# Reading the output projection's operands early, with SyncE in program order in the value slots of a hybrid mLSTM and forgetting-attention layer

## The chip, the cores and the metric

One core of a Trainium2 chip runs the whole layer in one launch. The metric is device time in microseconds, the median of three runs. TensorE is PE here, its weight loads PEld, VectorE DVE, ScalarE ACT, GpSimd POOL, and SyncE, which issues nearly all DMAs of this kernel, SP.

## The reference

A decoder layer on 1024 tokens of width 1024: four mLSTM heads and eight heads of forgetting attention side by side, then cross attention into 256 memory tokens, then a squared-ReLU MLP. The part around the change:

```python
def forgetting_attention(q, k, v, lf):
    ...
    def block(args):
        qi, ci, blk = args
        ...
        s = jnp.einsum('bqhd,bkhd->bhqk', qi, k, preferred_element_type=jnp.float32) * scale
        s = s + (ci[..., :, None] - cT[..., None, :])
        s = jnp.where(qpos[:, None] >= kpos[None, :], s, -jnp.inf)
        p = jax.nn.softmax(s, axis=-1)
        return jnp.einsum('bhqk,bkhd->bqhd', p.astype(v.dtype), v)
...
x = x + jnp.concatenate([ml_out, fx_out], axis=-1) @ w_out[l]
x = x + cross_attention(rmsnorm(x, ln_x[l]), rmsnorm(mem, ln_mem[l]), w_xq[l], w_xkv[l], w_xo[l])
```

## The kernel before

Everything is float32, and nearly every product is made in three passes of a reduced float32 type: each operand is split into a high part and a remainder (`split`: ACT copies the high part, DVE or POOL subtracts), and `mm3` (lines 190 to 194) multiplies low by high, high by low and high by high. PE's program is therefore long and almost without holes.

A planner orders the instructions of each engine before the launch, from estimated times. `in_order` (line 148) overrides it: the instructions traced inside such a block, on the four compute engines, are chained in the order of the program. Those of SP are not among them, so their order is the planner's. Each engine executes its own list strictly in order, and so does SP: an instruction that waits holds all behind it.

The part around the change has three steps.

**Leading slots** (line 1063). `score_parts` (line 833) gives the parts of the forgetting scores: for each of eight heads eight tiles of 128 queries, each tile of one or two parts of at most 512 keys, twelve parts a head. A slot (`slot`, line 998) takes one part: PE multiplies it (`Tile.score`, lines 754 and 755) into one of three `sc` banks. One slot later the mask is added (line 734) and DVE takes the maximum (`top`, line 761); two slots later ACT takes the exponential (`exp`, line 767), which frees the bank; three slots later POOL scales by the denominator (`scale`, line 778). Thirteen such slots run ahead of the value products, beside `token_major` (line 503), which projects the forgetting values in two halves of eight token tiles, and whose sink (line 661) stores them to DRAM (`fvd`).

**Value slots** (line 1076). 96 slots, each with one step of the value products: PE transposes one key tile of the probabilities (line 793), ACT and DVE split it (`cut`), and two slots later PE multiplies it with the values (line 813). In the same slot go the next score part, one read of `coming` (`fx_step`, line 725), stores of finished pairs of heads to `mix` (`fx_store`, lines 828 and 829), and filler work at a rate of 3.6 a slot (`filler`): first keys and values of the memory (`key_unit`, `value_unit`), which read the normalized memory `hm`, from slot 57 on the first part of the output projection (`out_unit`), for both halves of the tokens. The fillers' weights come through two raw buffers: `raw_load` (line 959) reads one, `cut_half` (lines 971 and 972) splits half of one a slot, and the next read into a buffer is issued when its cut is done. `coming` holds the stack reads of the head after next (`fx_load`, eight a head) and the residual `x` into `kept`, two a head.

**Drain** (line 1080). The slots without value products that follow, and then the rest of the filler.

The output projection's operand, `mix` (the outputs of the mLSTM heads and of the pairs of forgetting heads, high part and remainder), goes through DRAM. Units 0 and 4 of the first half read it (lines 927 and 928): four mLSTM heads at once with `mix_load`, two reads of 1 MB into an `act` buffer, of which there are seven, and one pair of forgetting heads with `mix_tile`, two reads of 256 KB into a `z4` buffer.

Of the kernel before, what the change touches and what calls it, by code (L numbers as in the profile page):

```python
# [9 lines left out]
F32 = mybir.dt.float32  # L10
F32R = mybir.dt.float32r
# [5 lines left out]
COMPUTE = (mybir.EngineType.PE, mybir.EngineType.Activation, mybir.EngineType.DVE, mybir.EngineType.Pool)  # L17
P = 128
T = 1024
TH = 512  # L20
D = 1024
KT = D // P
NM = 256
MLH = 4
FXH = 8
# [3 lines left out]
KX = 1  # L29
# [15 lines left out]
def hybrid_layer(ctx: ExitStack, tc: tile.TileContext, a: dict, out: bass.AP):  # L45
# [16 lines left out]
    def act(dt=F32R):  # L62
        return sb("act", [P, 8, TH], 7, dt)
# [12 lines left out]
    def z4():  # L76
        return sb("z4", [P, T + 3], 2)
# [33 lines left out]
    load = nc.sync.dma_start  # L111
# [33 lines left out]
    last_of = {}  # L145

    @contextmanager
    def in_order():

        traced = nc.cur_bb.bb.instructions  # L150
        last = traced[-1]
        yield
        start = next(k for k in reversed(range(len(traced))) if traced[k] is last) + 1
        for i in traced[start:]:
            if i.engine not in COMPUTE:
                continue
            if i.engine in last_of:
                tc.add_manual_dep(
                    i,
                    last_of[i.engine],  # L160
                    mybir.DependencyInfo(mybir.DependencyClass.NoSync, mybir.DependencyReason.DATA),
                    reason="in_order",
                )
            last_of[i.engine] = i.name
# [120 lines left out]
    hmd = dram.tile([P, 2, KT, NM], F32, name="hmd")  # L285
# [49 lines left out]
    for k in range(KT):  # L335
        if k % 2 == 0:
            c = slice(k % 4 * 256, k % 4 * 256 + 512)
# [44 lines left out]
    z, e, q, lf = (small[:, i:j].rearrange("p (t c) -> p t c", c=c) for i, j, c in ((0, 128, GC), (128, 224, GW), (224, 320, GW), (320, 416, GW)))  # L382
# [120 lines left out]
    def token_major(w_src, sink, cs=(0, 1), between={}, ready=()):  # L503

        for c in cs:
            ws = [both(ready.pop(0) if ready else weights(w_src[c, i]), lambda t: t.rearrange("p (k c) -> p k c", k=4)) for i in range(2)]
            for t in range(8):
                if t in between:
                    between[t]()
                hf, tt = divmod(t, 4)  # L510
                ps = mm()[:, 0:256]
                for k in range(KT):
                    x = both(h[hf], lambda z: z[:, k, tt * P : (tt + 1) * P])
                    mm3(ps, x, both(ws[k // 4], lambda z: z[:, k % 4]), k == 0, k == KT - 1)
                sink(t, c, ps)
# [59 lines left out]
    mix = dram.tile([2, 2, P, KT, TH], F32, name="mix")  # L575
# [83 lines left out]
    fvd = dram.tile([FXH, P, 8, 2 * FXD], F32, name="fvd")  # L659
# [6 lines left out]
    closing = iter(())  # L666
# [29 lines left out]
    closing = gates_then_memory()  # L696
    ready = ml_project(0)
    for hd in range(MLH):
        closing = ml_head(hd, *ready)
# [5 lines left out]
    for _ in range(2):  # L705
        t = act().rearrange("p a b -> p (a b)").rearrange("p (i c) -> p i c", i=4)
# [5 lines left out]
    coming = []  # L712
# [19 lines left out]
    def mask():  # L732
        while masks:
            nc.tensor.matmul(masks.pop(0), identb, causal, start=False, stop=True)
# [94 lines left out]
        load(mix[hf, 1, :, MLH + hd // 2], lo.bitcast(F32))  # L829

    rooms = {}

    def score_parts():

        for hd in range(FXH):
            for hf in range(2):
                if hf:
                    t = act(F32).rearrange("p a b -> p (a b)").rearrange("p (i c) -> p i c", i=4)
                    rooms[hd, hf] = [t[:, d, : (5 + d) * P] for d in range(4)]
                else:  # L840
                    t = [w4((P, 2, TH)) for _ in range(2)]
                    rooms[hd, hf] = [t[d // 2][:, d % 2, : (1 + d) * P] for d in range(4)]
                for d in range(4):
                    x = Tile(hd, 4 * hf + d, rooms[hd, hf][d])
                    for e in range(len(x.parts)):
                        yield x, e
            if hd + 2 < FXH:
                fx_load(hd + 2)
            if 0 < hd < 5:
                coming.extend((kept[:, n], a["x"][:, n, :TH]) for n in (2 * hd - 2, 2 * hd - 1))  # L850

    def fv_load(hd):
        t = w4((P, 8, P), F32R)
        load(t.bitcast(F32), fvd[hd])
        return t

    def value_steps():
# [14 lines left out]
    def mix_load(k0, k1, hf):  # L872
        t = act().rearrange("p (e k) c -> p e k c", e=2)
        for p_ in range(2):
            load(t[:, p_, : k1 - k0].bitcast(F32), mix[hf, p_, :, k0:k1])
        return [(t[:, 0, k], t[:, 1, k]) for k in range(k1 - k0)]

    def mix_tile(k, hf):
        t = z4()[:, :T].bitcast(F32R).rearrange("p (e c) -> p e c", e=2)
        for p_ in range(2):  # L880
            load(t[:, p_].bitcast(F32), mix[hf, p_, :, k])
        return t[:, 0], t[:, 1]

    late = []

# [34 lines left out]

        return [a["w_xv"][hd, i] for i in range(2)], run

    mixes = {}

    def out_unit(hf, n):
        def run(ws):
            if n == 0 and hf == 0 or n == 4 and hf == 0:
                mixes[n // 4] = mix_load(0, MLH, n // 4) + [mix_tile(k, n // 4) for k in range(MLH, MLH + KX)]
            x = kept[:, n]
            if hf:  # L930
                x = rotate("p", "b", "a", "p", "b")
                load(x, a["x"][:, n, TH:])
            w = both(ws[0], lambda t: t.rearrange("p (k c) -> p k c", k=MLH + KX))
            ps = mm()
            for k in range(MLH + KX):
                mm3(ps, both(w, lambda t: t[:, k]), mixes[hf][k], k == 0, k == MLH + KX - 1)
                yield 3.0, k == MLH + KX - 1, lambda: sink(x, ps)

        def sink(x, ps):
            v.tensor_tensor(out=x, in0=ps, in1=x, op=ALU.add)  # L940
            if hf:
                load(x1d[:, n], x)

        return [a["w_out_a"][n]], run
# [47 lines left out]
    scored, exped, adds, ended = [], [], [], []  # L992
# [2 lines left out]

    stores, topped = [], []

    def slot(values, until):
        with in_order():
            todo_ = late[:]  # L1000
            late.clear()
            closing = bool(ended)
            sums = []
            while ended:
                sums.append(fx_close(*ended[0]))
                hd, hf, _ = ended.pop(0)
                if hd % 2:
                    stores.append((hd, hf, True))
            x = next(steps_, None) if values else None
            if x:  # L1010
                x.turn()
            mask()

            while adds and not closing and len(adds) >= (LAG if x else 1):
                y = adds.pop(0)
                y.add()
                if y.last:
                    ended.append((y.hd, y.hf, y.ov))
                    break
            tops = scored[:]  # L1020
            scored.clear()
            for t, e in tops:
                t.top(e)
            if x:
                x.cut()
                adds.append(x)
            for f in sums:
                f()
            exps = topped[:]
            topped[:] = tops  # L1030
            for t, e in exps:
                t.exp(e)
            while exped:
                exped.pop(0).scale()
            exped.extend(t for t, e in exps if e == len(t.parts) - 1)
            fx_step()
            part = next(parts, None)
            if part:
                part[0].score(part[1])
                scored.append(part)  # L1040
            late.extend(filter(None, [f() for f in todo_]))
            if stores and stores[0][2]:
                stores[0] = (*stores[0][:2], False)
            elif stores:
                fx_store(*stores.pop(0)[:2])
            while spent[0] < until:
                step = next(fill, None)
                if step is None:
                    break
                spent[0] += step[0]  # L1050
                if step[1]:
                    late.append(step[2])
                    break
            n, e = divmod(halves[0], 2)
            if until and n < len(sources) and (e or sum(u >= now[0] for u, _ in sources[:n]) < 3):
                cut_half()
        return x
# [5 lines left out]
    for i in range(LEAD_):  # L1063
        slot(False, 0)
        if i in (1, 11):
            next(closing, None)
    token_major(a["w_fv"], fv_sink, between={4: lambda: next(closing, None)})
    hm = act().rearrange("p a b -> p (a b)").rearrange("p (e k c) -> p e k c", e=2, k=KT)
    kept = act(F32)
    load(hm.bitcast(F32), hmd)  # L1070
    banks[:] = ["mm", "m2"]
    raw_load()
    raw_load()
# [1 line left out]
    n = 0  # L1075
# [255 lines left out]
    for n in range(KT):  # L1331
# [7 lines left out]
        k = n % 4  # L1339
# [390 lines left out]
```

## Time and profile before

| | us |
|---|---|
| runs shown, median of three (lowest, highest) | 1522.5 (1521.36, 1523.13) |
| the profiled execution, its own time | 1519.66 |
| its span, first to last instruction | 1517.6 |
| PE busy in it | 1501.4 |
| DVE, ACT, POOL busy | 1103.2, 716.6, 438.5 |

An engine's row of the profile has its busy time, its share of the span and its instructions. A row of the waits has who waited, for whom, the total in us, how often, and the longest. A row of the order of time has the start, the duration, engine and line, operation, what is written and read, and in brackets how long the engine had been idle and what ended that. SPq is SP issuing a DMA: the row has the time of the issue, not of the transfer. Idle time below about 0.2 us isn't listed. The clock of PE was granted at 0.998 of its full rate on the mean of this execution.

### The profile page before, as it was taken

What the parts mean: (1) busy time and instruction counts of PE and PEld (TensorE: products, weight loads), DVE (VectorE), ACT (ScalarE), POOL (GpSimd) and SP (SyncE); (2) the same over time, 40 slices, a digit from 0 to 9 for tenths busy, and PEclk for the clock granted to TensorE, in tenths of its full rate; (3) what the DMA queues carried; (4) which work ended last, traced back from release to release, by engine and by line L of the source; (5) the groups of instructions that cost most, each with busy time, mean ns of one, the idle gap of its engine ahead of it and who ended that gap; (6) DMA issues with size and microseconds to landing.
All of it is one profiled execution on the core that took longest, in us unless ns stands there. A gap on an engine that the chain in (4) does not pass through costs nothing.

```text
span 1517.6 us, 21814 instructions
## 1 busy us (share of the span) xinstructions
PE 1501.4 (99%) x7708; PEld 1259.1 (83%) x7708; DVE 1103.2 (73%) x1741; ACT 716.6 (47%) x1345; POOL 438.5 (29%) x497
## 2 busy tenths in 40 slices
PE   9999999999999999999999999999999999999997
PEld 8888888889898888888888887788888888888887
DVE  7676676665798875844457888788887788777765
ACT  7343343334678763543443456565556432222124
POOL 0003030413455541011110033343333544333312
PEclk9999999999999999999999999999999999999999
DMA  6332323436897928634333436776775966555623
GB/s 212 112 115 89 118 100 124 133 125 179 253 296 225 310 89 285 228 108 130 124 110 126 163 122 237 276 276 238 273 254 215 364 260 222 222 222 214 256 85 111
DMA packets 113489, 288.32 MB, mean 190 GB/s; under 512 B 12626, under 2 KB 27276, under 8 KB 107236
## 3 DMA queue, kind: packets, MB, share of 16 engines
q1 hardware_dynamic: 113092, 286.82, 55.4%
q8 instruction: 60, 0.98, 0.3%
q14 instruction: 49, 0.40, 0.1%
q10 hardware_dynamic: 288, 0.11, 0.0%
HBM read 194.36 MB, written 92.53 MB: 189 GB/s over the span
## 4 chain that ended last, share of the span: by engine, by line
PE 61%; DVE 2%; DMA 2%; issue 1%; ACT 1%; POOL 1%; SPq 0%; POOLq 0%; DVEq 0%; ACTq 0%
PE sc L192 5%; PE sc L194 5%; PE sc L193 5%; PE tp L192 5%; PE tp L194 5%; PE tp L193 5%; PE m L193 4%; PE m L192 4%; PE m L194 4%; PE mm L193 4%; PE mm L192 4%; PE mm L194 4%; PE ov L192 2%; PE ov L194 2%; PE ov L193 2%
## 5 line engine op out<-in xcount | busy, mean ns | idle before, releaser
L193 PE MATMUL tp<-act,wh 128*128 128x512 f32 (+1 forms) x456 | 178.7, 392 | 0.0
L192 PE MATMUL tp<-act,wl 128*128 128x512 f32 (+1 forms) x456 | 178.6, 392 | 0.0
L194 PE MATMUL tp<-act,wh 128*128 128x512 f32 (+1 forms) x456 | 178.5, 392 | 0.0
L138 ACT ACTIVATE wh<-wr 128x1024 fp32r<-128x1024 f32 (+3 forms) x96 | 92.7, 967 | 98.4 <-PE tp L194 36.5
L139 DVE TENSOR_TENSOR wl<-wr,wh 128x1024 fp32r<-128x1024 f32 (+3 forms) x96 | 114.3, 1192 | 15.3 <-ACT wh L138 15.2
L192 PE MATMUL mm<-act,wl 128*128 128x512 f32 (+1 forms) x320 | 122.8, 384 | 0.0
L193 PE MATMUL mm<-act,wh 128*128 128x512 f32 (+1 forms) x320 | 122.5, 383 | 0.0
L194 PE MATMUL mm<-act,wh 128*128 128x512 f32 (+1 forms) x320 | 122.2, 382 | 0.0
L192 PE MATMUL m<-act,wl 128*128 128x512 f32 (+1 forms) x312 | 119.6, 383 | 0.3 <-DVE wl L139 0.3
L193 PE MATMUL m<-act,wh 128*128 128x512 f32 (+1 forms) x312 | 119.0, 381 | 0.7 <-DMA act<-mix 0.7
L194 PE MATMUL m<-act,wh 128*128 128x512 f32 (+1 forms) x312 | 119.0, 381 | 0.0
L192 PE MATMUL sc<-act,wl 128*128 128x512 f32 (+1 forms) x268 | 103.9, 388 | 0.0
L193 PE MATMUL sc<-act,wh 128*128 128x512 f32 (+1 forms) x268 | 103.7, 387 | 0.0
L194 PE MATMUL sc<-act,wh 128*128 128x512 f32 (+1 forms) x268 | 103.7, 387 | 0.0
L194 PEld LDWEIGHTS tp<-act,wh 128*128 128x128 f32 x456 | 85.7, 188 | 19.5
L192 PEld LDWEIGHTS tp<-act,wl 128*128 128x128 f32 x456 | 85.7, 188 | 19.1 <-DVE w L1374 0.3
L193 PEld LDWEIGHTS tp<-act,wh 128*128 128x128 f32 x456 | 85.8, 188 | 18.8
L1464 POOL TENSOR_TENSOR z<-wr 128x256 f32<-128x256 f32 x56 | 54.1, 986 | 147.1 <-DMA wr<-w_ff2q 135.2
L138 ACT ACTIVATE w<-wr 128x768 fp32r<-128x768 f32 (+2 forms) x31 | 25.5, 824 | 132.1 <-PE tp L194 69.1
L138 ACT ACTIVATE wh<-z 128x1024 fp32r<-128x1024 f32 (+2 forms) x55 | 52.5, 956 | 65.7 <-POOL z L1464 30.5
L139 DVE TENSOR_TENSOR wl<-z,wh 128x1024 fp32r<-128x1024 f32 (+2 forms) x55 | 65.9, 1199 | 11.3 <-ACT wh L138 11.2
L194 PEld LDWEIGHTS mm<-act,wh 128*128 128x128 f32 x320 | 60.1, 188 | 12.5
(673 smaller groups left out, 4197.3 us busy)
## 6 DMA issues: line engine op xcount, KB each, us to landing
act<-right SPq DMA_DIRECT2D x35, 1024.0 KB
right<-r_d SPq DMA_DIRECT2D x70, 256.0 KB
right<-w SPq DMA_DIRECT2D x56, 256.0 KB
wr<-w_ff2q SPq DMA_DIRECT2D x28, 512.0 KB
act<-fqk SPq DMA_DIRECT2D x48, 256.0 KB
wr<-w_in SPq DMA_DIRECT2D x20, 512.0 KB
wr<-w_ff SPq DMA_DIRECT2D x20, 512.0 KB
fqk<-r_p SPq DMA_DIRECT2D x32, 256.0 KB
```

The source lines that it names most:

```text
L138: s.activation(hi, src, AF.Copy)
L139: return v.tensor_tensor(out=lo, in0=src, in1=hi.bitcast(F32), op=ALU.subtract)
L192: nc.tensor.matmul(ps, w[1], x[0], start=first, stop=False, skip_group_check=more)
L193: nc.tensor.matmul(ps, w[0], x[1], start=False, stop=False, skip_group_check=more)
L194: nc.tensor.matmul(ps, w[0], x[0], start=False, stop=last, skip_group_check=more)
L1464: g.tensor_tensor(out=o, in0=x, in1=y, op=op)
```

## The change

Four edits, all around the slots:

- `in_order` takes the engines that it chains. In the leading and the value slots SP is among them; in the drain it is not.
- `score_steps` is what the slot did with maxima, exponentials and scaling, made a generator. `catch_up` runs it alone, with the mask, ahead of tiles 0 and 2 in both halves of the value projection.
- The reads of `mix` by the output units go into `coming`, one read of 256 KB a slot (`mix_ahead`): the first half's with heads 2, 3 and 4, the second half's with head 6. The residual reads are spread over heads 1, 4 and 5.
- The memory operand `hm`, one read of 2 MB, becomes two of 1 MB; the second is issued behind the first read of forgetting values.

```diff
-    def in_order():
+    def in_order(engines=COMPUTE):
...
-            if i.engine not in COMPUTE:
+            if i.engine not in engines:
...
-            if 0 < hd < 5:
-                coming.extend((kept[:, n], a["x"][:, n, :TH]) for n in (2 * hd - 2, 2 * hd - 1))
+            if hd == FXH - 2:
+                extra[hd].extend(mix_ahead(1))
+            coming.extend(extra[hd])
...
     def fv_load(hd):
         t = w4((P, 8, P), F32R)
-        load(t.bitcast(F32), fvd[hd])
+        x = load(t.bitcast(F32), fvd[hd])
+        if hd == 0:
+            with tc.issue_after(x.ins):
+                load(hm[:, :, KT // 2 :].bitcast(F32), hmd[:, :, KT // 2 :])
         return t
...
-    def mix_tile(k, hf):
-        t = z4()[:, :T].bitcast(F32R).rearrange("p (e c) -> p e c", e=2)
-        for p_ in range(2):
-            load(t[:, p_].bitcast(F32), mix[hf, p_, :, k])
-        return t[:, 0], t[:, 1]
+    mixes = {}
+
+    def mix_ahead(hf):
+        t = act().rearrange("p (e k) c -> p e k c", e=2)
+        z = [z4()[:, :T].bitcast(F32R).rearrange("p (e c) -> p e c", e=2) for _ in range(KX)]
+        mixes[hf] = [(t[:, 0, k], t[:, 1, k]) for k in range(MLH)] + [(y[:, 0], y[:, 1]) for y in z]
+        return [(mixes[hf][k][p_], mix[hf, p_, :, k]) for k in range(MLH + KX) for p_ in range(2)]
...
-            if n == 0 and hf == 0 or n == 4 and hf == 0:
-                mixes[n // 4] = mix_load(0, MLH, n // 4) + [mix_tile(k, n // 4) for k in range(MLH, MLH + KX)]
...
+    def score_steps():
+        tops = scored[:]
+        scored.clear()
+        for t, e in tops:
+            t.top(e)
+        yield
+        exps = topped[:]
+        topped[:] = tops
+        for t, e in exps:
+            t.exp(e)
+        while exped:
+            exped.pop(0).scale()
+        exped.extend(t for t, e in exps if e == len(t.parts) - 1)
+
+    def catch_up():
+        with in_order():
+            mask()
+            for _ in score_steps():
+                pass
+
     def slot(values, until):
-        with in_order():
+        with in_order(COMPUTE + (mybir.EngineType.SP,) * (values or not until)):
...
-    token_major(a["w_fv"], fv_sink, between={4: lambda: next(closing, None)})
+    token_major(a["w_fv"], fv_sink, between={0: catch_up, 2: catch_up, 4: lambda: next(closing, None)})
     hm = act().rearrange("p a b -> p (a b)").rearrange("p (e k c) -> p e k c", e=2, k=KT)
     kept = act(F32)
-    load(hm.bitcast(F32), hmd)
+    residual = [(kept[:, n], a["x"][:, n, :TH]) for n in range(KT)]
+    operands = mix_ahead(0)
+    for hd, more in ((1, residual[:4]), (2, operands[:4]), (3, operands[4:8]), (4, operands[8:] + residual[4:6]), (5, residual[6:])):
+        extra[hd].extend(more)
+    load(hm[:, :, : KT // 2].bitcast(F32), hmd[:, :, : KT // 2])
```

More of the change, by code (lines that the diff above doesn't have):

```diff
@@ L831, in hybrid_layer @@
     rooms = {}
+    extra = [[] for _ in range(FXH)]
     def score_parts():
@@ L921, in value_unit @@
         return [a["w_xv"][hd, i] for i in range(2)], run
-    mixes = {}
     def out_unit(hf, n):
         def run(ws):
-            if n == 0 and hf == 0 or n == 4 and hf == 0:
-                mixes[n // 4] = mix_load(0, MLH, n // 4) + [mix_tile(k, n // 4) for k in range(MLH, MLH + KX)]
             x = kept[:, n]
@@ L1019, in slot @@
                     break
[L1020 to L1023, printed above, removed]
+            going = score_steps()
+            next(going)
             if x:
@@ L1028, in slot @@
                 f()
[L1029 to L1035, printed above, removed]
+            next(going, None)
             fx_step()
```

## The prediction

> **What bounds the kernel now.** I read the page's head first, then the waits of PE between 285 and 600 us, then the busy time of each engine over successive groups of twelve slots, and last the order of time on each engine around every wait of PE.
>
> ```profile
> span 1517.6 us, 21814 instructions
> PE 1501.4 (99%) x7708; PEld 1259.1 (83%) x7708; DVE 1103.2 (73%) x1741; ACT 716.6 (47%) x1345; POOL 438.5 (29%) x497
> ```
>
> PE is busy for all but 16.2 us. The edits touch neither a product of PE nor its order, so they can only give back idle time of PE, or add to it. In the part that they touch, this is all of it that the profile lists:
>
> ```profile
> PE sc L754 <- ACT act L767: 2.5, 2, 1.8
> PE tp L793 <- DVE r_e L139: 1.5, 2, 0.9
> PE m L193 <- DMA act<-mix: 0.7, 1, 0.7
> PE sc L754 <- ACT w L767: 0.4, 1, 0.4
> PE tp L793 <- DVE w L139: 0.3, 1, 0.3
> ```
>
> The sum is 5.4 us. It is a ceiling on what can be gained from waits that the profile shows.
>
> ```profile
> L793 PE MATMUL tp<-ident,act x208: 270/272/329, 395.9 to 576.4; 128*128 128x128 f32 x104
> L793 PE MATMUL tp<-ident,w x80: 270/273/329, 391.3 to 563.5; 128*128 128x128 f32 x80
> 391.00:414.00 23.00, 21.03 (x154) 19.18 (x153) 19.75 (x46) 17.98 (x50) 10.74 (x17) 1.00 0.72 218
> 414.00:437.00 23.00, 22.93 (x175) 21.64 (x174) 20.83 (x50) 19.19 (x53) 12.85 (x18) 1.00 0.98 309
> 437.00:464.00 27.00, 24.96 (x185) 22.91 (x184) 23.33 (x56) 19.89 (x57) 13.97 (x21) 1.00 0.85 261
> 464.00:488.00 24.00, 24.00 (x186) 22.88 (x183) 21.07 (x51) 19.68 (x54) 12.82 (x20) 1.00 0.75 210
> 488.00:513.00 25.00, 23.69 (x166) 21.50 (x165) 21.86 (x58) 19.04 (x55) 13.68 (x24) 1.00 0.95 300
> 513.00:536.00 23.00, 23.00 (x135) 19.50 (x134) 19.22 (x46) 16.34 (x49) 11.43 (x19) 1.00 0.88 272
> 536.00:559.00 23.00, 23.00 (x135) 19.40 (x134) 20.05 (x49) 17.00 (x50) 10.77 (x18) 1.00 0.29 90
> ```
>
> The transposes of the probabilities (L793) mark the 96 value slots: from 391.3 to 576.4, about 1.94 us a slot. The windows are groups of about twelve slots; their columns are PE, PEld, DVE, ACT and POOL busy, clock, DMA share and GB/s. PE loses time in three of them: 2.0 us at the start, 2.0 us in the third, 1.3 us in the fifth. DVE is 84 to 91% busy throughout, the next bound once PE's waits are gone.
>
> **The change part by part.**
>
> *Leftover scores (catch_up).* Thirteen leading slots leave behind one mask and one maximum, the exponentials of the last two score parts and the scaling of two tiles. Today the first value slots do them:
>
> ```profile
> 388.71 0.47 ACT L141 ACTIVATE r_c<-tp,rcol 128x256 fp32r<-128x256 f32 x1 [2.59 <-DMA mix<-r_e]
> 391.54 0.47 ACT L141 ACTIVATE r_b<-m,rcol 128x256 fp32r<-128x256 f32 x1 [2.35 <-PE m L194]
> 391.78 0.29 DVE L761 TENSOR_REDUCE c_mx<-sc 128x1 f32<-128x128 f32 x1 [2.07 <-PE sc L734]
> 392.53 0.68 ACT L767 ACTIVATE act<-sc,c_mx 128x512 f32<-128x512 f32 x1
> 393.10 0.20 ACT L767 ACTIVATION_READ_ACCUMULATOR act<-sc,c_mx 128x1 f32 x1
> 393.20 0.29 ACT L769 ACTIVATE c_mx<-c_mx 128x1 f32<-128x1 f32 x1
> 393.36 0.44 PE L754 MATMUL sc<-act 128*128 128x384 f32 x1 [0.73 <-ACT act L767]
> 393.75 0.37 ACT L767 ACTIVATE w<-sc,c_mx 128x128 f32<-128x128 f32 x1
> 397.15 0.39 PE L754 MATMUL sc<-act 128*128 128x256 f32 x1 [0.38 <-ACT w L767]
> ```
>
> PE's next scores need one of three banks and wait 0.73 and 0.38 us for exponentials to free them. Moved beside the value projection, ACT's share (0.68 + 0.20 + 0.29 + 0.37 us, and a second accumulator read of about 0.20) is 1.7 us. ACT has idle stretches of 2.59 and 2.35 us there, and DVE one of 2.07, so nothing waits for it. Without that cover it would cost at most those 1.7 us, in front of the projection's sinks. I take a gain of 0.73 + 0.38 = 1.11 us; bounds: a loss of 1.7, and a gain of 2.0, all that the first window has.
>
> *SP in program order.* At present SP's order is the planner's. The largest wait of PE comes out of it:
>
> ```profile
> 448.49 0.86 DVE L972 TENSOR_TENSOR wl<-wr,wh 128x512 fp32r<-128x512 f32 x1 [0.37 <-ACT wh L971]
> 449.88 0.32 SPq L829 DMA_DIRECT2D mix<-r_f  x1
> SPq L881 <- DMA mix<-r_y: 2.4, 1, 2.4
> 452.65 0.32 SPq L881 DMA_DIRECT2D z<-mix  x1
> 453.07 0.37 SPq L959 DMA_DIRECT2D wr<-w_xv  x1
> 453.05 0.26 ACT L767 ACTIVATION_READ_ACCUMULATOR act<-sc,c_mx 128x1 f32 x1
> 457.06 0.63 ACT L971 ACTIVATE wh<-wr 128x512 fp32r<-128x512 f32 x1 [3.75 <-DMA wr<-w_xv]
> 458.68 0.50 PE L754 MATMUL sc<-act 128*128 128x512 f32 x1 [1.77 <-ACT act L767]
> ```
>
> The buffer of the raw weights was free at 448.49 + 0.86 = 449.35, yet w_xv is issued only at 453.07. In front of it stood the early read of the forgetting operand (z<-mix), waiting 2.4 us for the store of what it reads. ACT, in order, then sits 3.75 us at the weight cut, the exponentials behind it are late, and PE stands 1.77 us. In the changed order that read is no longer there (it moves to slots 56 and 57); w_xv follows the store of 449.88 and goes out near 450.3. With the same 3.99 us from issue to cut (453.07 to 457.06) the cut starts near 454.3, after a wait of about 1.0 us. Of the 3.75 us PE felt 1.77, so 1.98 us was slack, and 1.0 stays under it. Gain 1.77 us. What is late next is the remaining 0.26 + 0.65 us of waits for DVE, which I leave. Bounds: a gain of 2.7 (those too), and a loss by new stops of SP, priced with the rivals.
>
> The order also puts behind each waiting SP instruction whatever follows it in its slot: stack reads, stores of the memory keys and values, reads of raw weights. The stores wait for DVE and ACT work of the same slot, which stands ahead of the weight cut in DVE's own order too, so a raw read is not held by them: its buffer comes free later still. A stack read has about four slots, 8 us, before PE wants it.
>
> *Output operands early.* Twenty reads of 256 KB take the place of four of 1024 and four of 256, one a slot: the first half in slots 32 to 35, 44 to 47, 56 and 57, the second in 72 to 81.
>
> ```profile
> 422.71 3.15 SPq L728 DMA_DIRECT2D act<-x  x6
> 498.93 1.34 SPq L875 DMA_DIRECT2D act<-mix  x2
> 521.87 1.60 SPq L875 DMA_DIRECT2D act<-mix  x2
> 508.63 0.50 PE L193 MATMUL m<-act,wh 128*128 128x512 f32 x1 [0.67 <-DMA act<-mix]
> ```
>
> PE waits 0.67 us for the two reads issued at 498.93; in the new order their content has landed ten slots and more before. That is a gain of 0.67 us. The tightest piece is the forgetting operand, read in slots 56 and 57 and used in slot 60: three slots, 5.8 us, against the 3.99 us above. One slot late would cost 1.9, the other bound. Twelve more issues at about 0.35 us are 4 us of SP over 185, hidden. The bytes stay the same, but 4 MB leave the fifth and sixth window, where DMA was at 0.95 and 0.88, half of them for the third and fourth window (0.85 and 0.75), half for the seventh (0.29). The residual reads, six of them one after the other at 422.71 in the fullest window (0.98), spread out. PE was 22.93 of 23 busy there, so I book nothing.
>
> *Memory operand in two reads.*
>
> ```profile
> 377.90 0.56 SPq L1070 DMA_DIRECT2D act<-hmd  x1
> ```
>
> No wait of PE names it: issued at 377.90, first used after slot 4 begins near 396. The second read costs one more issue of 0.56 us on SP. Zero, and 0.56 either way.
>
> *Sum.* 1.11 + 1.77 + 0.67 = 3.55 us. The profiled execution took 1519.66 us, its span and 2.1 around it, and would take 1516.1; the median of the runs shown is 2.8 above it, so I forecast 1522.5 - 3.55 = 1519.0.
>
> **The rivals.**
>
> *SP becomes the head of the line (slower).* Place: raw reads (L959) in the value slots. If the strict order makes SP stop for a buffer or a landing ahead of a raw read, as z<-mix did, every such stop costs what that one cost, 1.77 us. Two eat the gain, four end at 1522.5 - 3.55 + 7.08 = 1526.0. For it: two raw buffers only, ACT in order, and by the code sixteen raw reads of key and value weights in the slots. Against: the waits in program order follow DVE's own order, as above.
>
> *DVE takes the time back.* At 84 to 91% DVE is close. If each of the three recoveries returns half as waits like the two of 0.9 us under r_e, the gain is 1.8 and the time 1520.7.
>
> *The leftovers are not done earlier.* If DVE and ACT reach them only when the projection ends, 1.11 is lost: 1520.1.
>
> *The smaller reads crowd the raws.* At 309 GB/s (window 414 to 437) 256 KB take 0.85 us of all DMA engines. Two of them ahead of a raw read in slots 32 to 47 raise ACT's wait from 1.0 to 2.7, 0.7 over the slack; at two places, 1.4: gain 2.1, 1520.4. [...]
>
> *More than the listed waits.* All 5.4 us go: 1517.1.
>
> **How the numbers follow.** Forecast 0.44, its own range 1517.5 to 1520.2; more 0.14; SP at the head of the line 0.17; DVE 0.12; leftovers 0.06; crowding 0.07. About 0.2%, 3.0 us, is what a measurement of this kernel can tell from no change: faster means under 1519.5, slower over 1525.5. Faster: 0.35 of the forecast's 0.44 and all of "more", 0.49. Slower: 0.14 of the SP rival's 0.17. The rest, 0.37, is the same. Range 1516.2 to 1524.5: below lies what unlisted gaps of PE could add to 5.4, above lies most of the SP rival.
>
> **What would show it.** Leftovers: the exponentials of the last leading parts stand before 391 and no score of the first six slots waits. SP order: no wait of ACT for w_xv over 2 us, and no z<-mix before slot 56. Operands: no wait of PE for mix. Wrong would be: a longer sum of PE's waits in the slots, ACT waiting for wr in several places, or idle time of PE under r_e beyond 1.5 us.

## The result, and the profile after

| | us, median (lowest, highest), runs | before beside it | ratio, 95% interval |
|---|---|---|---|
| the changed kernel | 1524.59 (1520.2, 1530.4), 22 | 1522.05 (1518.88, 1525.28), 22 | 1.0016 [1.0008, 1.0023] |

The change makes the kernel 2.5 us slower by the medians, where 3.5 us of gain had been forecast. The profiled execution took 1524.3 us, against 1519.66 before. The head of the profile after:

```profile
span 1522.6 us, 21823 instructions
PE 1502.7 (99%) x7708; PEld 1260.8 (83%) x7708; DVE 1098.4 (72%) x1741; ACT 717.2 (47%) x1345; POOL 444.8 (29%) x497
```

The waits of PE in it between 285 and 600 us:

```profile
PE sc L754 <- ACT act L767: 6.9, 3, 4.0
PE tp L793 <- DVE r_e L139: 0.4, 1, 0.4
PE tp L793 <- DMA act<-fqk: 0.3, 1, 0.3
PE tp L793 <- DVE w L139: 0.3, 1, 0.3
PE mm L192 <- DVE r_b L943: 0.2, 1, 0.2
```

Two waits of before are gone: the one for `mix` (0.7) and those for the leftover exponentials. But scores behind an exponential (L754 <- L767) now wait 6.9 us, not 2.5, so the listed sum rises from 5.4 to 8.1 us. Three of the groups of slots, in the columns of the rows before:

```profile
391.00:414.00 23.00, 19.95 (x146) 18.14 (x145) 17.25 (x38) 15.73 (x43) 8.65 (x13) 1.00 0.87 240
437.00:464.00 27.00, 22.70 (x169) 21.10 (x168) 21.17 (x48) 17.93 (x51) 13.45 (x20) 0.99 0.89 240
464.00:488.00 24.00, 24.00 (x173) 22.71 (x173) 19.72 (x52) 18.57 (x53) 11.88 (x19) 0.94 0.83 237
```

PE loses 3.1 us in the first (2.0 before) and 4.3 in the second (2.0). In the last it is busy throughout but does 173 matmuls, not 186: the granted clock is 0.94 there. The order of time on ACT, SP, DVE and PE around the two stalls of the changed kernel:

```profile
387.57 0.54 SPq L856 DMA_DIRECT2D w<-fvd  x1
388.16 0.61 SPq L859 DMA_DIRECT2D act<-hmd  x1
...
388.94 0.36 ACT L767 ACTIVATE w<-sc,c_mx 128x128 f32<-128x128 f32 x1
...
398.03 1.56 SPq L728 DMA_DIRECT2D act<-fqk  x2
401.81 0.36 SPq L962 DMA_DIRECT2D wr<-w_xk  x1
408.48 0.63 ACT L974 ACTIVATE wh<-wr 128x512 fp32r<-128x512 f32 x1 [3.62 <-DMA wr<-w_xk]
410.10 0.50 PE L754 MATMUL sc<-act 128*128 128x512 f32 x1 [2.63 <-ACT act L767]
...
449.98 0.86 DVE L975 TENSOR_TENSOR wl<-wr,wh 128x512 fp32r<-128x512 f32 x1 [0.36 <-ACT wh L974]
450.45 0.38 SPq L856 DMA_DIRECT2D w<-fvd  x1
450.88 0.46 SPq L728 DMA_DIRECT2D act<-fqk  x1
451.45 0.53 SPq L962 DMA_DIRECT2D wr<-w_xv  x1
460.83 0.63 ACT L974 ACTIVATE wh<-wr 128x512 fp32r<-128x512 f32 x1 [6.02 <-DMA wr<-w_xv]
462.45 0.50 PE L754 MATMUL sc<-act 128*128 128x512 f32 x1 [4.04 <-ACT act L767]
```

The last leftover exponential stands at 388.94, before 391 as forecast. Both stalls are raw weight reads that land late. w_xv goes out 0.6 us after its buffer is free (449.98 + 0.86 = 450.84), which is what the forecast wanted of the new order; but from issue to cut it takes 9.38 us, against 3.99 before. w_xk takes 6.67 us (401.81 to 408.48), and it is a wait that before did not have. Ahead of each stand reads of values and stacks, 512 and 256 KB each, and ahead of w_xk the first read of values and half of the memory operand too, issued at 387.57 and 388.16. While w_xk was on its way the DMA engines were full (in these rows the last two columns are the DMA share and GB/s):

```profile
402.00:406.00 4.00, 4.00 (x29) 3.65 (x27) 3.93 (x7) 2.62 (x8) 1.29 (x1) 1.00 1.03 214
```

In the kernel before, the same stretch had this:

```profile
402.00:406.00 4.00, 4.00 (x28) 3.62 (x28) 3.93 (x7) 3.38 (x9) 1.29 (x1) 1.00 0.42 138
```

### The profile page after: what moved, and what is told of

The parts are those of the page before. It is cut to its first block, busy times and chain, and to the rows that moved or that the text cites. A ratio compares the mean times of both kernels' runs of the same rounds, so it can differ in the third digit from the quotient of the medians.

```text
span 1522.6 us, 21823 instructions
## 1 busy us (share of the span) xinstructions
PE 1502.7 (99%) x7708; PEld 1260.8 (83%) x7708; DVE 1098.4 (72%) x1741; ACT 717.2 (47%) x1345; POOL 444.8 (29%) x497
## 4 chain that ended last, share of the span: by engine, by line
PE 87%; DVE 4%; DMA 4%; ACT 2%; issue 2%; POOL 1%; SPq 0%; POOLq 0%; DVEq 0%; ACTq 0%
PE tp L194 8%; PE tp L193 8%; PE tp L192 8%; PE m L192 6%; PE m L194 6%; PE m L193 6%; PE sc L192 6%; PE sc L194 6%; PE sc L193 6%; PE mm L192 5%; PE mm L193 5%; PE mm L194 5%; PE ov L192 2%; PE ov L193 2%; PE ov L194 2%; PE ov L813 2%
```

## The experiments

Each is a whole kernel, run beside the kernel before. A difference of 0.001 between ratios is 1.5 us.

**Taking the change apart.** e1: the changed kernel with SP's order left to the planner.

```diff
-        with in_order(COMPUTE + (mybir.EngineType.SP,) * (values or not until)):
+        with in_order():
```

> The changed kernel with SP's order in the slots left to the planner again; operands early, leftovers beside the value projection and the memory operand in two reads stay. Theory (program order of SP interleaves stack reads with raw weight reads, so that raw reads land late: 9.4 and 6.6 us instead of 4.0 and 3.4): the two PE waits of 2.6 and 4.0 us under the exponentials shrink to under 2 us together, the leftovers' 1.1 us stay won, and the time is 1 to 3 us below before and 3 to 6 below the changed kernel. Rival (the 256 KB operand reads crowd the raw reads whoever orders them): the waits near slots 33 to 36 stay over 3 us and the time is that of the changed kernel, 2 to 3 us above before.

Measured: 1522.94, ratio 1.0004 [0.9995, 1.0014]. From its order of time:

```profile
388.52 0.34 SPq L856 DMA_DIRECT2D w<-fvd  x1
395.21 0.73 PE L813 MATMUL ov<-r_e,w 128*128 128x512 f32 x1 [1.83 <-DMA w<-fvd]
```

Without SP's order the wait for w_xk is gone but PE waits for the first read of values, a wait that neither kernel has. Its issue is as late as in the changed kernel, so SP's order isn't what makes it late. The longest wait of PE that is left, 3.5 us, is the one behind w_xv: in the planner's order three of the operand reads (act<-mix, from 452.73) go out ahead of it, and it takes 5.88 us from issue to cut (455.02 to 460.90). So the theory's "under 2 us together" missed, and in this order the operand reads do crowd a raw read, as the rival has it.

e2: the kernel before, with SP in program order in the slots and nothing else of the change:

```diff
...
-        with in_order():
+        with in_order(COMPUTE + (mybir.EngineType.SP,) * (values or not until)):
```

> The kernel before with one edit: SP chained in program order in the leading and value slots; operands still read at the output units, 1 MB at a time. Theory: raw reads behind stack reads land late here too; PE waits under the exponentials of 4 us or more in all, 2 to 5 us above before. Rival (256 KB operand reads crowd the raws): no operand read before slot 56, so no long wait there, and the time is that of before or 1 to 2 us below it, since the early read that blocked SP at 450 is gone.

Measured: 1531.91, ratio 1.0058 [1.0046, 1.0070]. Its two longest waits of PE, in order of time:

```profile
514.85 0.77 PE L192 MATMUL m<-act,wl 128*128 128x512 f32 x1 [5.20 <-DMA act<-mix]
517.59 0.80 PE L193 MATMUL m<-act,wh 128*128 128x512 f32 x1 [1.97 <-DMA act<-mix]
```

In program order the bulk reads of `mix` go out (at 508.77) right ahead of their first use, and PE stands 7.2 us, which neither expectation named; under the exponentials it waits 2.9 us in all, where the theory had 4 or more. So the order costs time without the early operands. That it gains time with them is not shown by itself: e4 and e6 below, without and with it, are at 0.9991 and 0.9985, e7 and e8 at 0.9986 and 0.9982, and in both pairs the intervals overlap.

e3: the kernel before with the early leftovers (`score_steps`, `catch_up` and the new `between`) alone:

```diff
...
+    def catch_up():
+        with in_order():
+            mask()
+            for _ in score_steps():
+                pass
...
-    token_major(a["w_fv"], fv_sink, between={4: lambda: next(closing, None)})
+    token_major(a["w_fv"], fv_sink, between={0: catch_up, 2: catch_up, 4: lambda: next(closing, None)})
```

> The kernel before with one edit: the leftover scores finished beside the first value tiles. Theory: no wait of PE in the first two value slots, 1.1 us less idle time of PE there, 0.5 to 1.1 us below before. Rival (the leftovers displace the projection's sinks and the planner's order behind them): the same or 1 to 2 us above before.

Measured: 1528.64, ratio 1.0040 [1.0028, 1.0052]. From its order of time:

```profile
392.16 0.34 SPq L854 DMA_DIRECT2D w<-fvd  x1
399.39 0.80 PE L813 MATMUL ov<-r_e,w 128*128 128x512 f32 x1 [4.22 <-DMA w<-fvd]
```

The part that was forecast at +1.1 us of gain is the one that loses. The first read of values goes out at 392.16; PE waits 4.22 us for it. The rival had the direction, but not the size: by the ratio it is 6.1 us, not 1 to 2.

e4: the kernel before with the early operands and the spread residual alone:

```diff
-            if n == 0 and hf == 0 or n == 4 and hf == 0:
-                mixes[n // 4] = mix_load(0, MLH, n // 4) + [mix_tile(k, n // 4) for k in range(MLH, MLH + KX)]
...
+            if hd == FXH - 2:
+                extra[hd].extend(mix_ahead(1))
+            coming.extend(extra[hd])
```

> The kernel before with one edit: operands of the output projection and residual in the paced list, in 256 KB reads; SP's order is the planner's, the leftovers stay in the value slots, the memory operand is one read. Theory: PE's 0.67 us wait for mix is gone; the rest depends on where the planner puts the reads; within 1 us of before. Rival (256 KB reads crowd the raws): 2 us or more above before, with ACT waits for raw weights over 4 us.

Measured: 1520.87, ratio 0.9991 [0.9981, 1.0000]. The wait for `mix` is gone; the 0.67 us forecast for it lie inside the interval (0 to 2.9 us).

**The late first read of values.** Four kernels take the leftovers apart. e6: the changed kernel without `catch_up`:

```diff
-    token_major(a["w_fv"], fv_sink, between={0: catch_up, 2: catch_up, 4: lambda: next(closing, None)})
+    token_major(a["w_fv"], fv_sink, between={4: lambda: next(closing, None)})
```

> The changed kernel without the early leftovers (no catch_up), all else as in it. If the early leftovers are worth what the forecast gave them (1.1 us) here too: waits of 0.7 and 0.4 us come back at the first scores, the 4.04 us for w_xv stays between 3 and 4.5, and the time is 1525 to 1526.5. Rival, the early exponential takes a buffer the first value read needs, that read and the memory operand go out late and push w_xk's read: w<-fvd is issued near 371 instead of 387.6, the 2.63 us for w_xk falls to 1.0 or less, and the time is 1522.5 to 1523.7.

Measured: 1519.2, ratio 0.9985 [0.9975, 0.9996]: the rival was right in what it says of the reads, and the time is 3 us below its range. From its order of time:

```profile
449.21 0.53 SPq L962 DMA_DIRECT2D wr<-w_xv  x1
456.45 0.63 ACT L974 ACTIVATE wh<-wr 128x512 fp32r<-128x512 f32 x1 [3.70 <-DMA wr<-w_xv]
```

No wait of PE for w_xk is left, and the first read of values goes out at 370.28 again. The early leftovers cost the changed kernel 0.0031 of its time, 4.7 us. The wait for w_xv is as large as before: 3.70 us of ACT, 1.72 of PE.

e7: e4 with only the first of the two leftover steps (SP's order is the planner's). The exponential of part 12, the only one that writes a tile of the second forgetting head, stays in the first value slot:

```diff
...
+    caught = []
+
     def catch_up():
+        if caught:
+            return
+        caught.append(1)
         with in_order():
...
-    token_major(a["w_fv"], fv_sink, between={0: catch_up, 2: catch_up, 4: lambda: next(closing, None)})
+    token_major(a["w_fv"], fv_sink, between={0: catch_up, 4: lambda: next(closing, None)})
```

> Early operands alone (as in e4) with one of the two early leftover steps: the exponential of part 12, the only one that writes a buffer of the second forgetting head, stays in the first value slot. Theory, that exponential took the buffer which the first value read was to have: w<-fvd is issued near 371 as before, PE has no wait for it (4.22 us in e3, 1.83 in e1), the 0.73 us wait at the first scores goes, that of 0.38 may stay; time 1519.8 to 1520.5, e4 was 1520.9. Rival, the early leftovers delay that read in another way, by the work they move: a wait of 1.8 us or more for w<-fvd with half clock behind it stays, and the time is 1523 to 1528.

Measured: 1520.02, ratio 0.9986 [0.9977, 0.9995]; w<-fvd is issued at 371.56, no wait for it, none at the first scores. e8: the same edit on the whole changed kernel:

> The changed kernel with the exponential of part 12 left in the first value slot (the other early leftover steps stay). Theory, this one exponential takes the buffer of the first value read and so delays that read by 17 us and the memory operand's second half, the next stacks and w_xk behind it: w<-fvd is issued near 371, w_xk's read lands in under 4 us, the 2.63 us for w_xk is gone, no wait at the first scores but at most 0.4; time 1518.5 to 1520, e6 was 1519.2 with 0.7 more of waits there. Rival, the early leftovers cost time because the slots start in another phase against the reads: w<-fvd goes out early but the waits for w_xk and w_xv stay over 5 us in sum, time 1522.5 to 1525.

Measured: 1518.97, ratio 0.9982 [0.9973, 0.9991]. w<-fvd goes out at 370.45 and the wait for w_xk is gone. In e7 and e8 the first read and the time came out as the theory has them. Leaving one 0.36 us exponential where it was gives the changed kernel back 5 us.

Is it the exponential, or its place in the program? e11: the changed kernel, all leftovers early again, but the first read of values stands in the program ahead of that exponential:

```diff
+    def early_steps():
+        catch_up()
+        yield
+        first.append(fv_load(0))
+        catch_up()
+
+    first, early = [], early_steps()
-    token_major(a["w_fv"], fv_sink, between={0: catch_up, 2: catch_up, 4: lambda: next(closing, None)})
+    token_major(a["w_fv"], fv_sink, between={0: lambda: next(early, None), 4: lambda: next(closing, None)})
...
-        fvs = {0: fv_load(0)}
+        fvs = {0: first[0]}
```

The memory operand is one read again in this kernel, after the value projection.

> The changed kernel with all its early leftovers, but the first value read stands in the program ahead of the exponential of part 12 (and the memory operand is one read again, behind it). If the buffer is the cause and not the exponential: w<-fvd is issued near 371, w_xk's read lands in under 4.5 us, PE's 2.63 us for w_xk is gone, no wait at the first scores; what is left is one wait for w_xv of 1 to 2.3 us; time 1518 to 1520, as e8. If the early exponential itself is the cause (its time on ACT, or the phase it gives the slots): waits of over 5 us in sum as in the changed kernel, 1522.5 to 1525.

Measured: 1518.06, ratio 0.9981 [0.9971, 0.9991]. From its order of time:

```profile
370.68 0.38 SPq L856 DMA_DIRECT2D w<-fvd  x1
386.85 0.37 ACT L767 ACTIVATE w<-sc,c_mx 128x128 f32<-128x128 f32 x1
...
447.83 0.38 SPq L856 DMA_DIRECT2D w<-fvd  x1
448.27 0.45 SPq L728 DMA_DIRECT2D act<-fqk  x1
448.83 0.53 SPq L959 DMA_DIRECT2D wr<-w_xv  x1
455.25 0.63 ACT L971 ACTIVATE wh<-wr 128x512 fp32r<-128x512 f32 x1 [3.03 <-DMA wr<-w_xv]
456.88 0.50 PE L754 MATMUL sc<-act 128*128 128x512 f32 x1 [1.08 <-ACT act L767]
```

The exponential is early (386.85) and so is the read. So the place in the program decides, not the exponential's work; that the memory operand is one read here does not carry this, since e8, with two, is as fast. The tile that the exponential writes and the tile of that read are of one kind (`w4`, five buffers). The expectations say that it takes the read's buffer; that wording is too strong. In the changed kernel the read goes out 1.4 us before the exponential begins (387.57 and 388.94), so it did not wait for it on the chip: it stands later in SP's list. What fits the planned programs is that the planner hands out buffers of a kind in the program's order of first use, and puts the read some 250 instructions later where the exponential comes first. That rule is inferred from the plans, and no trace shows it; the effect of the place is shown.

**The reads ahead of a raw read.** e5: the changed kernel, but in each value slot the stack read and the read of values are issued behind the weight cut and the raw read that it releases:

```diff
-                    fvs[hd + 1] = fv_load(hd + 1)
+                    fvs[hd + 1] = w4((P, 8, P), F32R)
+                    behind.append((fvs[hd + 1].bitcast(F32), fvd[hd + 1]))
...
-            fx_step()
             part = next(parts, None)
...
                 cut_half()
+            while behind:
+                load(*behind.pop())
+            fx_step()
         return x
```

> The changed kernel, whole, but in each value slot the reads of stacks and of values (act<-fqk, w<-fvd) are issued behind the cut and the raw read it releases, not ahead of them. Theory A, raw reads land late because 0.75 MB of other reads was issued just ahead of them: w_xv's read lands within 5 us of its issue instead of 9.36, PE's 4.04 us there falls under 2 with no half clock behind it, the 2.63 us for w_xk under 1.2; the time is 1520.5 to 1522.5. Rival B, the engines are full there in any order: the landing stays 7 to 9 us, the waits over 3, the time 1524 to 1526. Rival C, a stack read that now stands behind a waiting raw read comes late: PE waits for act<-fqk at score matmuls, over 1525.

Measured: 1518.04, ratio 0.9969 [0.9957, 0.9981]. Of the waits of PE for an exponential this one is left:

```profile
PE sc L754 <- ACT act L767: 2.6, 1, 2.6
```

It is that for w_xk, at 409.81. No wait for w_xv is left in any slot: theory A holds there, against B and C. The one for w_xk stayed, where under 1.2 was expected: its delay starts at 387, ahead of the slots. Two more kernels, this edit with that of e8 (e9) and with that of e6 (e10), were to separate the two faults:

> Both corrections: the reads of stacks and values behind the raw read of their slot (as in e5) and the exponential of part 12 left in the first value slot. If the two faults are separate, e5's last stall (2.60 us for w_xk, with one window of half clock) goes as well: no wait of PE over 0.8 us in the slots, no half clock there, time 1514 to 1516. If they are one fault that either correction removes, 1517.5 to 1518.5.

> As the run before with all leftovers in the slots, as in the kernel before the change (e6 with raw reads first). Against it this shows what the early leftovers are worth where they delay no read: the waits of 0.7 and 0.4 us come back; 0.7 to 1.1 us longer than the run before, 1515 to 1517. Rival, nothing is left of them: the same time within 0.5 us.

Measured: 1519.82, ratio 0.9984 [0.9973, 0.9995], and 1517.80, ratio 0.9976 [0.9968, 0.9985]. Both times lie above what was expected, and neither tells what it was meant to. With `fx_step` behind the next part, the first stack read of the third head comes into the last leading slot and so, in SP's order, ahead of the first read of values. From the order of time of e10:

```profile
386.67 0.47 SPq L728 DMA_DIRECT2D act<-fqk  x1
387.90 0.55 SPq L856 DMA_DIRECT2D w<-fvd  x1
```

The read is late again, by another road, and e9 stalls 2.67 us for w_xk. e10 does not: with the leftovers in the slots w_xk goes out 1.2 us later (403.02, against 401.86), is at its cut after 4.71 us and not 6.72, and PE waits 0.7 us at most. Between 402 and 406 us the DMA share is 1.04 in e9 and 0.79 in e10. So a late first read of values is not enough for the stall. What fits is that w_xk must also go out while the engines are still full; no run moves w_xk alone. e12 corrects both faults: the program of e11, the raw read first in the value slots, `fx_step` left in its old place in the leading ones.

```diff
+            if not (values or until):
+                fx_step()
             going = score_steps()
...
+            while behind:
+                load(*behind.pop())
+            if values or until:
+                fx_step()
         return x
```

> As the run before, and in the value slots the reads of stacks and values stand behind the raw read of their slot; in the leading slots they stay where they were (in e5, e9 and e10 a stack read had come to stand ahead of the first value read and held it until 388). With both faults gone: w<-fvd near 371, w_xk and w_xv land within 5 us, no wait of PE over 0.9 us in the slots and no half clock there; time 1515.5 to 1517.5. If the orders of reads only trade one late read for another: a wait of over 1.5 us at another weight, 1518 to 1520.

Measured: 1515.61 (1515.06 to 1517.19, 5 runs), beside 1521.04 of the kernel before: ratio 0.9964 [0.9951, 0.9978]. The disputed read in its order of time:

```profile
450.29 0.53 SPq L960 DMA_DIRECT2D wr<-w_xv  x1
450.91 0.38 SPq L1072 DMA_DIRECT2D w<-fvd  x1
```

Its waits of PE for an exponential, and then its third group of slots:

```profile
PE sc L754 <- ACT act L767: 0.3, 1, 0.3
```

```profile
437.00:464.00 27.00, 26.73 (x203) 25.15 (x202) 25.37 (x60) 21.63 (x61) 15.34 (x25) 1.00 0.91 269
```

Of 6.9 us behind exponentials 0.3 are left, and the third group of slots is full: 203 matmuls, 169 in the changed kernel and 185 before. The first read of values goes out at 372.49. This version beats both kernels; e5, at 0.9969, is not clear of it.

## Why the prediction was wrong

*Leftover scores.* The step that failed is "nothing waits for it", with its lower bound of a loss of 1.7 us: it priced the moved instructions by their time on ACT alone. The waits at the first scores did go, as forecast (0.73 and 0.38). What was not asked is what the exponential of part 12 writes, and what else wants a tile of that kind. With it ahead of the first read of values in the program, that read goes out at 387.57, not near 370; behind it go the second half of the memory operand, stack reads and w_xk. In the order of reads of the changed kernel the price is 4.7 us (e6), not 1.1 of gain, and that is more than the whole slowdown. It is not a price that stands by itself, though: e5 keeps the early leftovers and the late read (387.70), and with the raw reads first it is 7.2 us below the changed kernel by the ratios. Either correction alone takes the slowdown away; both together (e12) give 7.9 us, not the sum. With the read traced first, the leftovers are worth 0.6 us by the ratios of e6 and e11 (0.9985 and 0.9981), less than their intervals tell from nothing.

*SP in program order.* The step that failed is "With the same 3.99 us from issue to cut". The early issue came true: 449.21 without the leftovers, 448.83 with the read ahead, against 453.07. But what went out ahead of w_xv changed with it: a read of values and one of a stack, 0.75 MB, at 447.83 and 448.27, where before one read of 256 KB (z<-mix, 452.65) stood just ahead. From issue to cut it took 7.24 and 6.42 us, and PE still waited 1.72 and 1.08. The 1.77 us were there to be had: with the raw read first in its slot that wait is gone, and the ratio falls from 0.9981 (e11) to 0.9964 (e12), 2.6 us. The two intervals overlap, but nine of the eleven runs of e11 are longer than the longest of e12's five.

*Rivals.* "The smaller reads crowd the raws" named the mechanism but saw only the operand reads in slots 32 to 47 and priced a place at 0.7 us; in the changed kernel the crowding came from reads that were there before, in another order. With the planner's order (e1 and e4) operand reads did stand just ahead of w_xv. "SP becomes the head of the line" was half right: no stop of SP held w_xv, which left 0.6 us after its buffer was free, but SP's order alone did cost 0.0058, in the bulk reads of `mix`, which the early operands remove. "DVE takes the time back" did not come: the waits under r_e fell from 1.5 to 0.4 us. (Of the two before, which the prediction calls "of 0.9 us", one was 0.87 and the other 0.65.) Nor were the leftovers late: the last exponential stands at 388.94.

e5 moves the same reads in the same sizes as the changed kernel, and e12 as e11; PE's wait for w_xv, 4.04 us in the changed kernel and 1.08 in e11, goes away by order alone.

*Operands early.* Right: the wait for `mix` is gone, the operands alone are at 0.9991, a gain at the edge of the interval. *Memory operand in two reads.* Not tried alone. By e6 it costs nothing that shows where the first read of values is early; in the changed kernel its second half is chained to that read and is late with it.

*What a stall costs.* The sum priced every stall at PE's idle time, 1.77 us a stop, since the edits could "only give back idle time of PE, or add to it". In the changed kernel 1.7 us more follow, 3.41 us at a granted clock of 0.50; the last section shows them. They complete the account of the two profiled executions: listed waits +2.7, clock +1.7, and 0.6 for the rest make the 5.0 us between the spans. The forecast also carried the 2.8 us between the profiled execution of the kernel before and the median along as if they were fixed. They go with the clock, in part: the 88 runs of the kernel before beside the experiments take 1521.0 and 1520.9 us on the mean at a granted clock of 0.998 and 0.997, 1522.6 at 0.996 and 1524.5 at 0.995. So the listed waits do not bound what the median can gain: those of e12 are 2.9 us shorter than before, its median is 5.4 us shorter, and four of its five runs have 0.998.

*Left open.* Why the two corrections do not add up was not found. The nine microseconds of w_xv in the changed kernel are more than the 6.4 and 7.2 that the same two reads ahead gave in other kernels. While it waited, the queues moved little with all engines busy (columns as above). The changed kernel:

```profile
458.00:460.00 2.00, 0.41 (x2) 0.00 (x0) 0.00 (x0) 0.00 (x0) 0.35 (x1) 1.00 1.01 188
```

The kernel before, while it waited for the same weight:

```profile
456.00:458.00 2.00, 0.91 (x7) 0.47 (x4) 0.47 (x1) 0.94 (x2) 1.07 (x3) 1.00 1.01 375
```

A full share carried 188 GB/s here and 375 there. What made the packets slow was not found.

## What to carry to other kernels

When work is moved ahead, ask what it writes as well as how long it takes: here one exponential, moved ahead, made the planner place the read into a tile of the same kind later; the read went out 17 us late, and the loss showed some 20 us after that, at another engine. A read that others wait for should stand first among the reads of its step; issuing it 4 us earlier was worth nothing here while bulk reads left just ahead of it (PE still waited 1.72 us for w_xv in e6, against 1.77 before). And price a wait by what the clock does behind it, not by its idle time alone: in e1 3.42 us at 0.50 stood behind a wait of 1.83.

## What the hardware showed

Behind a stall of 1.83 us in e1 the granted clock of PE was 0.50 for 3.42 us, behind the one of 4.04 us in the changed kernel for 3.41. In e1 two low stretches start at 395.30 and at 463.57, 68.27 us apart, about twenty times 3.41. The rows below have that length. The first number after the length is PE busy, the third from the end the granted clock. The changed kernel, around its stall of 4.04 us:

```profile
459.97:463.38 3.41, 0.93 (x6) 0.84 (x6) 1.12 (x2) 2.55 (x8) 1.27 (x1) 1.00 0.79 198
463.38:466.79 3.41, 3.41 (x15) 3.02 (x14) 3.28 (x9) 2.72 (x9) 0.97 (x2) 0.50 0.65 179
```

e1, around the 1.83 us at its first values:

```profile
391.89:395.30 3.41, 1.15 (x8) 0.63 (x6) 2.44 (x6) 1.53 (x5) 0.00 (x0) 1.00 1.03 349
395.30:398.72 3.42, 3.42 (x10) 2.78 (x11) 0.96 (x3) 0.84 (x3) 0.35 (x2) 0.50 1.04 298
```

e4, around a stall of 1.96 us for w_xv:

```profile
455.60:459.01 3.41, 1.63 (x13) 1.18 (x11) 1.49 (x5) 1.44 (x4) 1.84 (x3) 1.00 0.97 362
459.01:462.42 3.41, 3.23 (x20) 2.67 (x21) 3.00 (x9) 3.25 (x12) 0.54 (x1) 1.00 1.05 405
```

e5, behind its stall of 2.60 us for w_xk:

```profile
409.70:413.11 3.41, 3.30 (x14) 3.10 (x14) 2.99 (x9) 2.11 (x7) 0.47 (x1) 0.50 0.39 112
413.11:416.53 3.42, 3.42 (x26) 3.23 (x25) 2.56 (x8) 2.44 (x8) 1.58 (x5) 1.00 0.37 134
```

e9, around its stall of 2.67 us for w_xk:

```profile
406.10:409.51 3.41, 1.43 (x11) 0.98 (x10) 1.70 (x5) 0.93 (x2) 1.86 (x3) 1.00 0.45 147
409.51:412.93 3.42, 2.73 (x10) 2.54 (x11) 2.82 (x6) 2.69 (x9) 1.04 (x1) 0.50 0.30 109
412.93:416.34 3.41, 3.41 (x14) 2.96 (x13) 1.45 (x5) 1.13 (x4) 1.51 (x4) 0.50 0.56 183
```

A row with 0.93, 1.15 or 1.43 us of PE work was followed by one at 0.50, and so was a stretch with 1.47 in e2 (457.11 to 460.53, with a stall of 1.95 us in it; its row from 459.01 to 462.42 has a clock of 0.72). The row of e4 with 1.63 was not: the next has 1.00. Whether PE's busy time is what decides is not shown. Of the rows at 0.50 that of e5 with 3.30 us busy was followed by one at 1.00, that of e9 with 2.73 by another at 0.50.

So the stall of 1.83 us in e1 costs nearly as much again, by an estimate from the row behind it: half of 3.42 us. Three stalls of nearly one length for w_xk were followed by different clocks: the 2.63 us of the changed kernel at 410 by no low row, the 2.60 us of e5 by one and the 2.67 us of e9 by two. The author's estimate is that the place counts: counted back from 463.38 in sixteen steps of 3.41 us, a step ends near 408.8, inside the stall of the changed kernel, and PE was busy for 2.12 us from 405.36 to 408.77 and for 2.08 from there to 412.18, both at a clock of 1.00. It would fit the spread of the changed kernel's 22 runs over 10 us: the three with a clock of 0.997 or 0.998 took 1520.2 to 1521.4 us, the three with 0.993 took 1526.8 to 1530.4. That the place made this difference is not shown, since one execution of each kernel was profiled.
